# Extended-block loads issued from ScalarE's queue, the transposed inverse copied by VectorE, and new planner costs in a hybrid delta-rule encoder layer

## The chip, the cores and the metric

The kernel runs on one core of one Trainium2 chip. A core has a matrix engine (TensorE, "PE" in the profile; its weight loads are listed apart as "PEld"), three engines for elementwise work (VectorE "DVE", ScalarE "ACT", GpSimd "POOL") and SyncE ("SP"), which here does nothing but issue DMA transfers. [...] The metric is the device time of one execution in microseconds, the median of several executions. The profile is one further execution.

## What is computed

One encoder layer in fp32 on 512 tokens of width 1024: an RMS norm, one combined projection, a pooling branch, a gated delta rule run forward and backward over 8 heads, a merge by two gates, an output projection, and a feed-forward part with a width-3 convolution (inner width 2816). The change touches the delta rule. Cut to that:

```python
def gated_delta_rule(q, k, v, g, beta):      # chunks of 64 tokens, per head
    ...
    kb = k * beta[..., None]
    vb = v * beta[..., None]
    L = jnp.where(strict, jnp.einsum('bhnid,bhnjd->bhnij', kb, k) * decay, 0.0)
    rhs = jnp.concatenate([kb * jnp.exp(G)[..., None], vb], axis=-1)
    sol = lax.linalg.triangular_solve(L + eye, rhs, left_side=True, lower=True,
                                      unit_diagonal=True)
    ...
    s0 = jnp.zeros((B, H, dk, dv), jnp.float32)
    _, o = lax.scan(step, s0, xs)            # the state goes from chunk to chunk

    o_f = gated_delta_rule(qc, kc, vc, g_f, beta_f)
    flip = lambda t: jnp.flip(t, axis=1)
    o_b = flip(gated_delta_rule(flip(qc), flip(kc), flip(vc), flip(g_b), flip(beta_b)))
```

## The kernel before, in words

**Products.** Tokens lie in four tiles of 128. Every large product is fp32 split into a high and a low half: for each slab of 128 weight rows TensorE makes three products, high by high (L371), low activations by high weights (L372) and high activations by low weights (L373), each 512 columns wide. The weights come as `wr_*` blocks by DMA; ScalarE casts the high half `wh_*` (L392), GpSimd makes the low half `wl_*` (L396).

**The order.** `Planner` collects all tasks with the buffers that they read and write, a key and a cost for each engine, and simulates the engines with these costs: ring buffers come free when their last reader ends, and each engine takes the ready task with the lowest key. The simulated order becomes the program of each engine; at run time every engine goes through its own list in order and waits for semaphores. So a cost in the planner sets no duration, but it does set the order. `MM3` is the planner's cost of the three products of a slab, `FOUR` that of one group of small products in the delta rule (`pk`, `pw`, `su` and others). `L` (L273) makes a load task; all of them go to SyncE.

**The triangular solve.** The eight heads go through it in two groups of four. `inv_unit` (L863 on) inverts all 32 x 32 diagonal blocks of a group at once: the blocks are loaded as `rw`, copied as `n` (L882) and `un` (L887) by ScalarE, and thirty elimination steps run on VectorE (L897, L901), ended by a memset (L908). `back` (L912 to L914) then copies the result on ScalarE out of PSUM, `un`, into two SBUF blocks: `inv` as it stands, and `rev` with the two inner axes exchanged. Four stores (L920) put halves of them into two scratch arrays in DRAM, `u_scr` and `e_scr`. `spread_unit` (L924 on) reads them back in another layout: four loads of the extended blocks `ext` from `e_scr` and four of `nm` from `u_scr` (L941), 128 KB each. `merge_unit` (L948 on) joins the 32-wide inverses into 64-wide ones with small 32 x 32 products: `l1a` (L959) reads `nm` and `ext`, then come `l1b` (L970), `l1t` (L977) and a second level. The delta steps follow: `pw` (L1136), `su` (L1151), `o`.

Between these, the planner lets TensorE do the products of the combined projection as fillers: `ps_gd` (merge gate), `ps_k`, `ps_v`, `ps_q`, `ps_p` (pooling), `ps_gp`. Their results are convolved (`cv_*`, L747 on ScalarE, L753 on VectorE, L763 and L765 on ScalarE) or copied out (`sgd`, L1201; `pool_p`, L1290).

**The head.** `pe_warm` (L572 to L574) runs transposes of an identity that nobody reads; `spread_n1` (L563) broadcasts the norm's weights as `n1b`; `norm_transpose` (L511 on) scales (`xs`, L522) and transposes (`pt_a`, L533) a token tile.

Of the kernel before, what the change touches and what calls it, by code (L numbers as in the profile page):

```python
# [196 lines left out]
    return 0.17 + n * 0.0023  # L197


MM3, FOUR = 0.665, 0.9  # L200
TABLES = {
    "sqrt": "sqrt_and_others",
    "exp": "natural_log_exp_and_others",
# [6 lines left out]
def hybrid_block(  # L210
# [23 lines left out]
    pe, act, dve, pool, sp = nc.tensor, nc.scalar, nc.vector, nc.gpsimd, nc.sync  # L234
# [13 lines left out]
    add = plan.add  # L248
    table = {"now": "sqrt"}

    def with_table(tab, fn):
        def run():
            if table["now"] != tab:
                table["now"] = tab
                if TABLES[tab]:
                    act.preload_act_table_set(TABLES[tab])
            fn()

        return run

    def A(cost, fn, r=(), w=(), key=0.0, tab=None):
        add("act", cost, with_table(tab, fn) if tab else fn, r, w, key, tab)
# [7 lines left out]
    def M(cost, fn, r=(), w=(), key=0.0):  # L270
        add("pe", cost, fn, r, w, key)

    def L(kb, fn, r=(), w=(), key=0.0, after=(), land=Planner.LAND):  # L273
        add("sp", Planner.ISSUE, fn, r, w, key, kb=kb, after=after, land=land)

    def Z(fn, r=(), w=(), key=0.0, after=()):
        add("none", 0.0, fn, r, w, key, after=after)
# [8 lines left out]
    def bank(tag, name):  # L286
        return psum.tile([P, 512], F32, tag=tag, bufs=RINGS[tag], name=name)
# [283 lines left out]
    def pe_warm(n):  # L571
        pt = bank("ds", f"pt_warm{n}")  # L572
        for i in range(n):
            pe.transpose(pt[:, 0:P], ident, ident)  # L574
# [291 lines left out]
    def inv_unit(g):  # L866
        c = CHAIN + 1000 * g + 400
        b = {}
        fl = lambda t_: t_.rearrange("u r c -> u (r c)")
        hi_, lo_ = slice(64, 128), slice(0, 64)  # L870
        block = lambda n: ring("dp", "x4", (P, B32, B32), F32, f"{n}_{g}")

        def blocks(scr, d):
            return scr.rearrange("b h d t r c -> d (b h) t (r c)")[d]

        Z(lambda: b.update(n=block("n")), r=["pool:dp"], w=[f"x4:n{g}"], key=c)
        Z(lambda: b.update(rw=block("rw")), r=["pool:dp"], w=[f"x4:rw{g}"], key=c)
        L(256, lambda: sp.dma_start(fl(b["rw"][lo_]), blocks(b_scr[g], 0)), r=[f"bscr{g}"], w=[f"x4:rw{g}"], key=c)  # L880
        L(256, lambda: sp.dma_start(fl(b["n"][hi_]), blocks(b_scr[g], 1)), r=[f"bscr{g}"], w=[f"x4:n{g}#1"], key=c)
        A(1.1, lambda: act.copy(b["n"][lo_], b["rw"][lo_].rearrange("p r c -> p c r")),  # L882
          r=[f"x4:rw{g}"], w=[f"x4:n{g}#0"], key=c)

        def take():
            b["un"] = banks2(f"un_{g}", (P, B32, B32))
            act.copy(b["un"], b["n"])  # L887

        A(1.1, take, r=[f"x4:n{g}"], w=[f"oo:un{g}"], key=c)

        def step(k):
            un = b["un"]
            n = B32 - 1 - k
            if k == 1:
                b["tmp"] = ring("dp", "x2", (P, 256), F32, f"tmp_{g}")
            tm = b["tmp"][:, 0 : n * k].rearrange("p (r c) -> p r c", c=k)
            dve.tensor_tensor(  # L897
                out=tm, in0=b["n"][:, k + 1 :, k : k + 1].to_broadcast([P, n, k]),
                in1=un[:, k : k + 1, 0:k].to_broadcast([P, n, k]), op=ALU.mult,
            )  # L900
            dve.tensor_tensor(out=un[:, k + 1 :, 0:k], in0=un[:, k + 1 :, 0:k], in1=tm, op=ALU.add)  # L901

        for k in range(1, B32 - 1):
            V(0.44 + 2 * 0.00105 * (B32 - 1 - k) * k, lambda k=k: step(k),
              r=[f"x4:n{g}"], w=[f"oo:un{g}", f"x2:tmp{g}"], key=c)

        def end():
            dve.memset(fl(b["un"])[:, 0 : B32 * B32 : B32 + 1], 1.0)  # L908

        V(0.2, end, w=[f"oo:un{g}"], key=c)  # L910

        def back(n):  # L912
            b[n] = block(n)
            act.copy(b[n], b["un"] if n == "inv" else b["un"].rearrange("p r c -> p c r"))  # L914

        for n in ("inv", "rev"):
            A(1.1, lambda n=n: back(n), r=[f"oo:un{g}"], w=[f"x4:{n}{g}"], key=c)
        for n, rows, scr, d in (("inv", hi_, "u", 1), ("inv", lo_, "e", 0), ("rev", lo_, "u", 0), ("rev", hi_, "e", 1)):
            dst = u_scr if scr == "u" else e_scr
            L(256, lambda n=n, rows=rows, dst=dst, d=d: sp.dma_start(blocks(dst[g], d), fl(b[n][rows])),  # L920
              r=[f"x4:{n}{g}"], w=[f"{scr}scr{g}#{d}"], key=c, land=3.6)


    def spread_unit(g):  # L924
        c = CHAIN + 1000 * g + 590
        q = [slice(i * B32, (i + 1) * B32) for i in range(4)]

        def zero():
            extg[g] = ring("dp", "ext", (P, HG, 2, NT, 64), F32, f"ext_{g}")
            pool.memset(extg[g][q[0], :, 0, :, 32:64], 0.0)  # L930
            pool.memset(extg[g][q[3], :, 1, :, 0:32], 0.0)
            for h in range(g * HG, (g + 1) * HG):
                exts[h] = extg[g][:, h % HG]

        G(2.0, zero, r=["pool:dp"], w=[f"ext:{g}"], key=c)

        def load(b_, ext):
            scr = (e_scr if ext else u_scr)[g][b_].rearrange("h d t r c -> r (h d t) c")
            o = B32 * (b_ % 2)
            dst = extg[g][q[b_], :, :, :, o : o + B32] if ext else nmg[g][q[b_], :, :, :, q[b_]]  # L940
            sp.dma_start(dst.rearrange("r h d t c -> r (h d t) c"), scr)  # L941

        for b_ in range(4):
            L(128, lambda b_=b_: load(b_, True), r=[f"escr{g}", f"ext:{g}"], w=[f"exl{g}#{b_}"], key=c, land=4.0)
            L(128, lambda b_=b_: load(b_, False), r=[f"uscr{g}", f"bscr{g}", f"nm:{g}"], w=[f"nml{g}#{b_}"], key=c, land=4.0)


    def merge_unit(h):  # L948
# [445 lines left out]
        L(256, lambda: sp.dma_start(g_scr["m1"][c], b["t"]), r=[f"y:lgp{c}"], w=[f"gscrm1{c}"], key=u - 300)  # L1394


    M(4.0, lambda: pe_warm(12), w=["ds:warm0"], key=-9e6)
    A(1.3, lambda: act.preload_act_table_set("sqrt_and_others"), key=-9e6)
    for t, k in ((0, -9e6), (1, -8.9e6), (2, FEED + 240), (3, FEED + 250)):
        L(512, lambda t=t: load_x(t), w=[f"st:x{t}"], key=k)  # L1400
    L(4, load_n1, w=["st:n1"], key=-8.95e6)
    M(2.0, spread_n1, r=["st:n1"], w=["oo:n1"], key=-8.9e6)
    for t in range(NT):
        norm_transpose(
            -8e6 + t, lambda t=t: xin[t], [f"st:x{t}"], lambda: [lambda: n1["bc"][:, 0, :], lambda: n1["bc"][:, 1, :]], ["oo:n1", "oo:n1"],
            lambda: h_hi, lambda: h_lo, "h", t,
            lambda t=t: ring("st", "xs", (P, D), F32, f"xs_{t}"), f"xs:{t}", f"a{t}", None,
        )
# [8 lines left out]
    def swap_st():  # L1417
# [5 lines left out]
      after=[f"st:x{t}" for t in range(NT)] + ["st:n1", "par"] + [f"xs:{t}" for t in range(NT)])  # L1423
# [93 lines left out]
    for t in range(NT):  # L1517
        L(512, lambda t=t: sp.dma_start(x2[t], xt[t * P : (t + 1) * P, :]), r=["pool:xp"], w=[f"xr{t}#0", f"xr{t}#1"],
          key=unit["n"] * 100, after=[f"pp:do{1 + t}"])
    L(512, lambda: sp.dma_start(pools["n2b"], norm2_w[0].partition_broadcast(P)), r=["pool:xp"], w=["n2b"],  # L1520
      key=unit["n"] * 100, after=["pp:do5"])
# [48 lines left out]
    for i, (t, hf) in enumerate(order):  # L1570
        u = next_unit()
        b = {}
# [112 lines left out]
    for c in range(NF):  # L1685
        b = {}
# [275 lines left out]
```

## Time and profile before

| | us |
|---|---|
| median of three executions | 896.82 |
| lowest and highest of them | 896.58, 899.38 |
| the profiled execution | 899.88 |
| its span from first to last instruction | 898.1 |
| time outside that span | 1.78 |
| mean granted TensorE clock (1 is full) | 0.992 |

In a row of the timeline or the chain, the first number is the start in us from the start of the span and the second the duration; then come engine, line, operation, output and inputs. In brackets stands the idle time of the engine just before and what ended it. "x26" is 26 instructions of the kind in one row, and the duration then is from the first start to the last end. Matmuls overlap: the end of one is modelled and lies behind the start of the next, so TensorE's pace is read from the distance of the starts. "SPq" is SyncE's instruction queue, and the duration there is that of issuing a transfer, not that of the transfer.

### The profile page before, as it was taken

What the parts mean: (1) busy time and instruction counts of PE and PEld (TensorE: products, weight loads), DVE (VectorE), ACT (ScalarE), POOL (GpSimd) and SP (SyncE); (2) the same over time, 40 slices, a digit from 0 to 9 for tenths busy, and PEclk for the clock granted to TensorE, in tenths of its full rate; (3) what the DMA queues carried; (4) which work ended last, traced back from release to release, by engine and by line L of the source; (5) the groups of instructions that cost most, each with busy time, mean ns of one, the idle gap of its engine ahead of it and who ended that gap; (6) DMA issues with size and microseconds to landing.
All of it is one profiled execution on the core that took longest, in us unless ns stands there. A gap on an engine that the chain in (4) does not pass through costs nothing.

```text
span 898.1 us, 14074 instructions
## 1 busy us (share of the span) xinstructions
PE 880.4 (98%) x5169; PEld 739.0 (82%) x5169; DVE 551.6 (61%) x978; ACT 462.1 (51%) x791; POOL 502.7 (56%) x447
## 2 busy tenths in 40 slices
PE   8999999999999998999999999999999999999996
PEld 7888888788987886889788888888888888888885
DVE  4757596157986785555434243665655554569996
ACT  5688644345867443334864433444443333465663
POOL 3445455223665553244567905787778774567772
PEclk9999999999999998999999999999999999999998
DMA  7364446613355357112698605666666554366563
GB/s 204 96 204 128 129 119 173 132 25 105 96 141 132 115 147 126 41 48 82 203 314 283 207 26 180 210 214 208 205 226 211 199 199 124 112 199 198 168 198 117
DMA packets 176266, 140.20 MB, mean 156 GB/s; under 512 B 32111, under 2 KB 143548, under 8 KB 176197
## 3 DMA queue, kind: packets, MB, share of 16 engines
q1 hardware_dynamic: 175620, 138.25, 51.3%
q10 hardware_dynamic: 576, 1.05, 0.3%
q8 instruction: 41, 0.67, 0.3%
q14 instruction: 29, 0.23, 0.1%
HBM read 114.08 MB, written 25.20 MB: 155 GB/s over the span
## 4 chain that ended last, share of the span: by engine, by line
PE 82%; DVE 9%; DMA 3%; issue 2%; SPq 2%; ACT 1%; POOL 0%; ACTq 0%; DVEq 0%; POOLq 0%
PE ps_up L372 9%; PE ps_up L373 9%; PE ps_up L371 9%; DVE as L1630 2%; PE ps_k L371 2%; PE ps_k L372 2%; PE ps_k L373 2%; PE ps_wo L373 2%; PE pw L1136 2%; PE ps_wo L372 2%; PE ps_wo L371 2%; PE ps_z L373 2%; PE ps_do L373 2%; PE ps_do L372 2%; PE ps_z L372 2%
## 5 line engine op out<-in xcount | busy, mean ns | idle before, releaser
L396 POOL TENSOR_TENSOR wl_up<-wr_up,wh_up 128x512 fp32r<-128x512 f32 x88 | 113.4, 1310 | 51.5 <-ACT wh_up L392 51.3
L372 PE MATMUL ps_up<-h_lo,wh_up 128*128 128x512 f32 (+1 forms) x368 | 139.9, 380 | 0.3 <-DVE h_lo L541 0.3
L371 PE MATMUL ps_up<-h_hi,wh_up 128*128 128x512 f32 (+1 forms) x368 | 139.9, 380 | 0.0
L373 PE MATMUL ps_up<-h_hi,wl_up 128*128 128x512 f32 (+1 forms) x368 | 139.7, 380 | 0.0
L1676 DVE SCALAR_TENSOR_TENSOR c<-ps_up,fw,c 128x511 f32<-128x511 f32 x88 | 66.0, 750 | 100.7 <-ACT c L1670 98.8
L1661 POOL TENSOR_TENSOR tp<-tp 128x512 f32<-128x512 f32 x44 | 61.8, 1404 | 41.7 <-DMA tp<-in_ffn_down_dram 35.7
L1864 POOL TENSOR_TENSOR w_dn<-wr_dn,w_dn 128x512 fp32r<-128x512 f32 x44 | 67.5, 1550 | 26.7 <-ACT w_dn L1861 22.8
L372 PEld LDWEIGHTS ps_up<-h_lo,wh_up 128*128 128x128 f32 x368 | 69.2, 188 | 13.7 <-DVE h_lo L541 0.5
L373 PEld LDWEIGHTS ps_up<-h_hi,wl_up 128*128 128x128 f32 x368 | 69.2, 188 | 13.1
L371 PEld LDWEIGHTS ps_up<-h_hi,wh_up 128*128 128x128 f32 x368 | 69.2, 188 | 13.0
L392 ACT CAST wh_up<-wr_up 128x1024 fp32r<-128x1024 f32 x44 | 46.3, 1051 | 62.3 <-issue 22.3
L1861 ACT CAST w_dn<-wr_dn 128x512 fp32r<-128x512 f32 x69 | 42.3, 621 | 28.7 <-PE dn L373 20.2
L372 PE MATMUL dn<-w_dn,as 128*128 128x512 f32 x141 | 54.2, 385 | 0.0
L371 PE MATMUL dn<-w_dn,as 128*128 128x512 f32 x141 | 54.2, 384 | 0.0
L373 PE MATMUL dn<-w_dn,as 128*128 128x512 f32 x141 | 54.2, 384 | 0.0
L1630 DVE TENSOR_TENSOR as<-a,as 128x512 fp32r<-128x512 f32 (+1 forms) x41 | 42.3, 1057 | 0.1
L1626 ACT CAST as<-a 128x512 fp32r<-128x512 f32 (+1 forms) x41 | 21.5, 534 | 33.0 <-DVE a L1697 28.4
L396 POOL TENSOR_TENSOR wl_k<-wr_k,wh_k 128x512 fp32r<-128x512 f32 x16 | 20.1, 1282 | 29.0 <-ACT wh_k L392 25.8
L396 POOL TENSOR_TENSOR wl_gd<-wr_gd,wh_gd 128x512 fp32r<-128x512 f32 x16 | 21.5, 1368 | 25.4 <-ACT wh_gd L392 23.8
L396 POOL TENSOR_TENSOR wl_gp<-wr_gp,wh_gp 128x512 fp32r<-128x512 f32 x16 | 21.6, 1372 | 22.4 <-ACT wh_gp L392 18.0
L1670 ACT ACTIVATE c<-ps_up,fw 128x512 f32<-128x512 f32 x44 | 33.9, 770 | 0.0
L1699 ACT ACTIVATE c<-c 128x512 f32<-128x512 f32 x22 | 13.9, 633 | 35.1 <-DVE c L1676 35.1
(361 smaller groups left out, 2455.8 us busy)
## 6 DMA issues: line engine op xcount, KB each, us to landing
wr_up<-in_ffn_up_dram SPq DMA_DIRECT2D x44, 512.0 KB, 3.9
tp<-in_ffn_down_dram SPq DMA_DIRECT2D x22, 512.0 KB, 4.8
t_scr<-tp SPq DMA_DIRECT2D x44, 256.0 KB, 3.1
wr_dn<-t_scr SPq DMA_DIRECT2D x20, 512.0 KB, 3.8
wr_dn<-in_ffn_down_dram SPq DMA_DIRECT2D x15, 512.0 KB, 3.6
x<-in_x_dram SPq DMA_DIRECT2D x8, 512.0 KB, 5.3
wr_k<-in_w_in_dram SPq DMA_DIRECT2D x8, 512.0 KB, 6.0
wr_z<-in_w_in_dram SPq DMA_DIRECT2D x8, 512.0 KB, 3.8
```

What stands on the lines that cost most here:

```text
L371: pe.matmul(ps, ahi, bhi, start=first, stop=False)
L372: pe.matmul(ps, ahi, blo, start=False, stop=False)
L373: pe.matmul(ps, alo, bhi, start=False, stop=last)
L392: act.copy(b["hi"], b["raw"])
L396: pool.tensor_tensor(out=b["lo"][:, sl], in0=b["raw"][:, sl], in1=f32(b["hi"][:, sl]), op=ALU.subtract)
L1626: act.copy(sets[p][:, i : i + n, 0, :], src())
L1630: dve.tensor_tensor(out=w[:, :, 1, :], in0=src(), in1=f32(w[:, :, 0, :]), op=ALU.subtract)
L1661: G(cp(512), lambda o=o, x=x, y=y: pool.tensor_tensor(out=w(*o), in0=w(*x), in1=w(*y), op=ALU.subtract), r=[n(*x), n(*y)], w=[n(*o)], key=u)
L1670: act.activation(b[j], box["ps"], AF.Identity, scale=fw[:, 1, ci : ci + 1], bias=fw[:, 3, ci : ci + 1])
L1676: dve.scalar_tensor_tensor(out=y[:, lo:hi], in0=box["ps"][:, lo + sh : hi + sh], scalar=fw[:, k, ci : ci + 1], in1=y[:, lo:hi], op0=ALU.mu ...
L1861: act.copy(b["w"][:, 0, :], raw["t"][:, j, :])
L1864: eng.tensor_tensor(out=b["w"][:, 1, :], in0=raw["t"][:, j, :], in1=f32(b["w"][:, 0, :]), op=ALU.subtract)
```

## The change

Five edits, all in the planner's input:

- The planner's cost of the three products goes from 0.665 to 0.682 us, and `FOUR` from 0.90 to 0.88.
- `L` takes an engine and an issue cost. The four `ext` loads of each group are issued by ScalarE's queue, with a planner cost of 1.0; the four `nm` loads stay on SyncE, at 1.1 (0.45 before).
- `rev` is copied by VectorE instead of ScalarE; `inv` stays.
- `pe_warm(12)` becomes `pe_warm(13)`, with a planner cost of 2.6 instead of 4.0.
- A second `pe_warm(8)` is added, keyed between the first and the `n1b` products that it now precedes (`spread_n1` has a key of -8.9e6, but waits for the load of the weights).

```diff
-MM3, FOUR = 0.665, 0.9
+MM3, FOUR = 0.682, 0.88
...
-    def L(kb, fn, r=(), w=(), key=0.0, after=(), land=Planner.LAND):
-        add("sp", Planner.ISSUE, fn, r, w, key, kb=kb, after=after, land=land)
+    def L(kb, fn, r=(), w=(), key=0.0, after=(), land=Planner.LAND, issue=Planner.ISSUE, eng="sp"):
+        add(eng, issue, fn, r, w, key, kb=kb, after=after, land=land)
...
         def back(n):
             b[n] = block(n)
-            act.copy(b[n], b["un"] if n == "inv" else b["un"].rearrange("p r c -> p c r"))
-
-        for n in ("inv", "rev"):
-            A(1.1, lambda n=n: back(n), r=[f"oo:un{g}"], w=[f"x4:{n}{g}"], key=c)
+            if n == "inv":
+                act.copy(b[n], b["un"])
+            else:
+                dve.tensor_copy(b[n], b["un"].rearrange("p r c -> p c r"))
+
+        for n, E in (("inv", A), ("rev", V)):
+            E(1.1, lambda n=n: back(n), r=[f"oo:un{g}"], w=[f"x4:{n}{g}"], key=c)
...
-            sp.dma_start(dst.rearrange("r h d t c -> r (h d t) c"), scr)
+            (act if ext else sp).dma_start(dst.rearrange("r h d t c -> r (h d t) c"), scr)
...
-            L(128, lambda b_=b_: load(b_, True), r=[f"escr{g}", f"ext:{g}"], w=[f"exl{g}#{b_}"], key=c, land=4.0)
-            L(128, lambda b_=b_: load(b_, False), r=[f"uscr{g}", f"bscr{g}", f"nm:{g}"], w=[f"nml{g}#{b_}"], key=c, land=4.0)
+            L(128, lambda b_=b_: load(b_, True), r=[f"escr{g}", f"ext:{g}"], w=[f"exl{g}#{b_}"], key=c, land=4.0, issue=1.0, eng="act")
+            L(128, lambda b_=b_: load(b_, False), r=[f"uscr{g}", f"bscr{g}", f"nm:{g}"], w=[f"nml{g}#{b_}"], key=c, land=4.0, issue=1.1)
...
-    M(4.0, lambda: pe_warm(12), w=["ds:warm0"], key=-9e6)
+    M(2.6, lambda: pe_warm(13), w=["ds:warm0"], key=-9e6)
...
     M(2.0, spread_n1, r=["st:n1"], w=["oo:n1"], key=-8.9e6)
+    M(1.6, lambda: pe_warm(8), w=["ds:warm1"], key=-8.8e6)
```

With the new costs the planner makes a new order on every engine. The number of 512-wide products on TensorE stays the same, and ScalarE's order holds 30 loads of activation tables instead of 28. In the rows of the order below, a name's number counts up in the order in which buffers are made, `L944` in the new kernel is `L941` in the old, and `L915` is `L914`.

Where the elimination of heads 0 to 3 is prepared, ScalarE had, before the change:

```order
L763 ACTIVATE cv_v_1223<-cv_v_1223 128x512
L392 CAST wh_z_1265<-wr_z_1106 128x1024
L1189 ACTIVATE zo_1276<-ps_z_1211 128x512
L882 COPY n_376<-rw_377 64x1024
L887 COPY un_1291<-n_376 128x1024
L1077 ACTIVATE v_1296<-pt_v_1271,rki 128x128 x4
```

After it, the same engine at the same place:

```order
L392 CAST wh_q_1221<-wr_q_1075 128x1024
L747 ACTIVATE cv_v_1230<-ps_v_1164,cw 128x512
L882 COPY n_386<-rw_387 64x1024
L887 COPY un_1265<-n_386 128x1024
L392 CAST wh_z_1274<-wr_z_1147 128x1024
L1192 ACTIVATE zo_1288<-ps_z_1225 128x512
```

The two copies that VectorE's elimination needs now precede the cast of a `z` weight and the activation of its product.

Where that inverse is copied out, ScalarE had:

```order
L765 ACTIVATE qT_1574<-cv_q_1524 128x512
L914 COPY inv_1611<-un_1291 128x1024
L392 CAST wh_gd_1621<-wr_gd_1498 128x1024
L747 ACTIVATE cv_v_1634<-ps_v_1554,cw 128x512
L914 COPY rev_1640<-un_1291 128x1024
L392 CAST wh_gd_1667<-wr_gd_1547 128x1024
L1201 COPY sgd_1673<-ps_gd_1617 128x512
```

and has now:

```order
L915 COPY inv_1561<-un_1265 128x1024
L765 ACTIVATE qT_1585<-cv_q_1548 128x512
L392 CAST wh_gd_1591<-wr_gd_1466 128x1024
L1204 COPY sgd_1607<-ps_gd_1534 128x512
L944 DMA ext_391<-e_scr_101 32x32x32
L392 CAST wh_gd_1644<-wr_gd_1525 128x1024
L747 ACTIVATE cv_v_1654<-ps_v_1587,cw 128x512
L944 DMA ext_391<-e_scr_101 32x32x32 x3
L392 CAST wh_gd_1688<-wr_gd_1578 128x1024
```

`rev` has left this engine, and the four `ext` loads are issued from it, one before a weight's cast and three after the convolution behind that cast. On TensorE the first `l1a` of this group follows 498 of the 512-wide products instead of 528.

For heads 4 to 7, SyncE issued the loads before the change in this order:

```order
L387 DMA wr_gp_3459<-in_w_in_dram 128x8x128
L920 DMA e_scr_102<-rev_3443 16x4x1024
L941 DMA nm_2695<-u_scr_100 32x32x32 x3
L387 DMA wr_p_3511<-in_w_in_dram 128x8x128
L941 DMA nm_2695<-u_scr_100 32x32x32
L941 DMA ext_2118<-e_scr_102 32x32x32 x4
```

Now ScalarE has them, in these rows:

```order
L392 CAST wh_gp_3487<-wr_gp_3365 128x1024
L1293 COPY pool_p_3448<-ps_p_3436 128x512
L944 DMA ext_2056<-e_scr_102 32x32x32 x4
L392 CAST wh_p_3545<-wr_p_3417 128x1024
L1080 ACTIVATE v_3551<-pt_v_3493,rki 128x128 x4
```

The four stand between the copy of `pool_p` and the cast of the next pooling weight. The first `l1a` of this group follows 1061 wide products instead of 1067.

## What I predict

> **What bounds the kernel now.** I read the page's totals first, then the chain that ended last, then the waits of TensorE.
>
> ```profile
> span 898.1 us, 14074 instructions
> PE 880.4 (98%) x5169; PEld 739.0 (82%) x5169; DVE 551.6 (61%) x978; ACT 462.1 (51%) x791; POOL 502.7 (56%) x447
> PE 82%; DVE 9%; DMA 3%; issue 2%; SPq 2%; ACT 1%; POOL 0%; ACTq 0%; DVEq 0%; POOLq 0%
> ```
>
> TensorE is busy for 98% of the span, and the change alters neither the count nor the shape of its weight products; only small transposes at the start are added. So the time can move only where TensorE waits, where its clock is low, or where it does those transposes. The waits are few:
>
> ```profile
> PE l1a L959 <- DMA ext<-e_scr: 4.7, 4, 1.7
> ...
> PE pt_a L533 <- DVE xs L522: 0.9, 1, 0.9
> ```
>
> Of the times in each row (total, count, longest), the first is the largest: `l1a`, the first small products of the merge, waits for the extended blocks that the change loads from another queue. Around those waits the windows (length, busy time of PE, PEld, DVE, ACT, POOL, then granted clock, DMA share, GB/s) show a second loss.
>
> ```profile
> 164.00:170.00 6.00, 4.34 (x42) 3.30 (x41) 0.00 (x0) 1.80 (x3) 2.49 (x2) 0.72 1.00 243
> 344.00:355.00 11.00, 7.97 (x127) 5.44 (x126) 5.32 (x8) 2.70 (x7) 3.53 (x5) 0.69 0.77 129
> 815.00:885.00 70.00, 70.00 (x319) 58.08 (x318) 69.90 (x79) 45.48 (x85) 51.12 (x32) 1.00 0.52 167
> ```
>
> The granted clock is 0.72 and 0.69 around the two waits, and 1.00 in the down projection, where TensorE and VectorE are both full. TensorE's own rows give the size of it. Heads 0 to 3 first:
>
> ```profile
> 162.77 0.39 PE L372 MATMUL ps_gd<-h_lo,wh_gd 128*128 128x512 f32 x1
> 163.00 0.39 PE L373 MATMUL ps_gd<-h_hi,wl_gd 128*128 128x512 f32 x1
> ...
> 165.98 0.43 PE L959 MATMUL l1a<-ext,nm 32*32 32x32 f32 x26 [1.66 <-DMA ext<-e_scr]
> 166.34 0.79 PE L371 MATMUL ps_k<-h_hi,wh_k 128*128 128x512 f32 x1
> ...
> 169.07 0.63 PE L371 MATMUL ps_k<-h_hi,wh_k 128*128 128x512 f32 x1
> ...
> 169.83 0.40 PE L373 MATMUL ps_k<-h_hi,wl_k 128*128 128x512 f32 x1
> ```
>
> Starts are 0.23 us apart before the wait. The eight starts from 166.34 to 169.83 take 3.49 us where 8 x 0.23 = 1.84 would do: 1.65 us lost to the clock. Heads 4 to 7:
>
> ```profile
> 345.48 0.22 PE L959 MATMUL l1a<-ext,nm 32*32 32x32 f32 x2 [0.48 <-DMA ext<-e_scr]
> 347.20 0.32 PE L959 MATMUL l1a<-ext,nm 32*32 32x32 f32 x4 [1.50 <-DMA ext<-e_scr]
> 348.56 0.63 PE L959 MATMUL l1a<-ext,nm 32*32 32x32 f32 x26 [1.04 <-DMA ext<-e_scr]
> 349.12 0.80 PE L371 MATMUL ps_p<-h_hi,wh_p 128*128 128x512 f32 x1
> ...
> 351.98 0.49 PE L970 MATMUL l1b<-nm,x 32*32 32x32 f32 x20
> ...
> 352.88 0.80 PE L371 MATMUL ps_p<-h_hi,wh_p 128*128 128x512 f32 x1
> ...
> 354.28 0.45 PE L959 MATMUL l1a<-ext,nm 32*32 32x32 f32 x32
> ```
>
> Three waits, 0.48 + 1.50 + 1.04 = 3.02 us; then six products take 2.86 (349.12 to 351.98) instead of 1.38, and three take 1.40 instead of 0.69: 2.19 us to the clock.
>
> The Trainium skill, TensorE: Matmul & The Clock Gate, Part 1 (The HAM clock gate), speaks against the clock's share: the gate falls back only after an idle window of about 3.4 us. By that rule a pause like the first would cost its wait alone, and the sum would gain the waits without the slow stretch behind the first. The rows above disagree: after 1.66 us of waiting, eight starts take 3.49 us.
>
> **The change part by part.** *Heads 0 to 3.* Rows of ScalarE and VectorE, of the chain, and of the loads (their issue in ns, minimum, median, maximum, and the time to landing):
>
> ```profile
> 108.92 2.07 ACT L882 COPY n<-rw 64x1024 f32<-64x1024 f32 x1
> ...
> 144.42 1.01 ACT L914 COPY inv<-un 128x1024 f32<-128x1024 f32 x1 [1.50 <-DVE un L908]
> 147.11 1.05 ACT L392 CAST wh_gd<-wr_gd 128x1024 fp32r<-128x1024 f32 x1 [1.68 <-PE ps_v L372]
> 148.07 0.68 ACT L747 ACTIVATE cv_v<-ps_v,cw 128x512 f32<-128x512 f32 x1
> 148.65 1.01 ACT L914 COPY rev<-un 128x1024 f32<-128x1024 f32 x1
> 152.64 1.05 ACT L392 CAST wh_gd<-wr_gd 128x1024 fp32r<-128x1024 f32 x1 [2.99 <-PE ps_gd L372]
> ```
> ```profile
> 112.08 0.20 DVE L897 TENSOR_TENSOR tmp<-n,un 128x30 f32<-128x30 f32 x1 [6.49 <-ACT un L887]
> ...
> 144.88 1.88 DVE L1063 TENSOR_TENSOR dt<-pkq,dt 128x512 f32<-128x512 f32 x3
> ```
> ```profile
> 150.24 3.37 DMA e_scr<-rev
> ...
> 160.68 5.26 DMA ext<-e_scr
> ```
> ```profile
> L941 SPq DMA_DIRECT2D ext<-e_scr x8: 554/900/2221, 155.1 to 343.7; - x8
> ...
> DMA to landing us min/median/max: 4.2/5.1/5.5
> ```
>
> `rev` stood on ScalarE behind `inv`, a weight cast that waits for TensorE, and a convolution: it began 4.2 us after `inv`. On VectorE it follows the inverse directly. No row shows this copy there. Three 512-wide operations of VectorE take 1.88 us, so 1024 elements are 1.25 us; the bounds are ScalarE's 1.01 for the same copy and 2.07 for its transposed `n`. I take 1.25, the row of the same engine. What it delays there is VectorE's own next work, which waits on nothing that TensorE awaits at once: nothing charged.
>
> With the finish where it was, `rev` would be done at 144.4 + 1.25 = 145.7 instead of 149.7, its second store land at about 147.2 + 3.4 = 150.6, four loads at the median issue of 0.90 go until 154.2, and the last land near 159.3. But the order also puts `n` ahead of a weight's cast and its product's activation, and VectorE had waited 6.49 us for that chain before its first elimination step: I expect the inverse 2 to 6 us sooner, and the last load landed between 153 and 157. ScalarE has room to issue it: three of the four stand where `rev` was, from 148.7, before the idle 2.99 us that end at 152.64. TensorE comes to `l1a` sooner as well: 30 fewer 512-wide products stand ahead, 30 x 0.23 = 6.9 us, so it is there at 157.1 instead of 164.0. The wait is 0 at the expected finish and 2.2 with the finish where it was; I take 0, so all of it goes: **-1.66**, and with it the clock's **-1.65**. What is late next is the loads that stay on SyncE: their last was issued after the last extended one before, but four issues are gone from between them.
>
> *Heads 4 to 7.*
>
> ```profile
> 329.79 1.02 ACT L914 COPY rev<-un 128x1024 f32<-128x1024 f32 x1
> ...
> 333.85 0.58 ACT L1290 COPY pool_p<-ps_p 128x512 f32<-128x512 f32 x1
> ```
> ```profile
> 332.72 1.43 SPq L920 DMA_DIRECT2D e_scr<-rev  x1
> ...
> 339.90 4.77 SPq L941 DMA_DIRECT2D ext<-e_scr  x4
> ```
>
> Here the four extended loads were the last on SyncE, from 339.90 on. On ScalarE they stand behind the copy of `pool_p`, over at 334.4; the store of `rev` that they need, issued at 332.7 before, comes sooner with `rev`. Issued at 0.55 to 1.2 each (4.77 / 4), the last goes by 336.6 to 339.2 and lands 5.1 later, at 341.7 to 344.3. TensorE has 6 products fewer ahead, 1.4 us, so it is at `l1a` at 343.4 instead of 344.8. The wait is 0 to 0.9; I take 0: **-3.02**, and **-2.19** of clock.
>
> *The four issues on ScalarE* cost it 4 x 0.90 = 3.6 us a group. They lie beside TensorE's products as long as the casts behind them are early: the cast of 152.64 ends at 153.69, and its 24 products are the last before 164.0, so they begin near 158.5. That is 4.8 us of cover, less what GpSimd needs for the low half. I charge nothing; without that cover it would be 3.6 a group.
>
> *The head.*
>
> ```profile
> 1.63 2.82 PE L574 MATMUL pt_warm<-ident 128*128 128x128 f32 x12 [1.63 <-POOL ident masks.py:199]
> 4.38 3.78 PE L563 MATMUL n1b<-n1row,ones 1*128 1x512 f32 x4
> ...
> 9.71 1.41 DVE L522 SCALAR_TENSOR_TENSOR xs<-x,nst_a,n1b 128x512 f32<-128x512 f32 x2
> ```
>
> Twelve transposes hold TensorE from 1.63 to 4.38, 0.23 each; 21 would end 9 x 0.23 = 2.1 later, at 6.4, and the broadcast of the norm's weights starts then. If the clock is released by then, its 3.78 halves, as 3.49 against 1.84 does for products, to 1.9, and it ends at 8.3 instead of 8.2: about 0, or -0.3 where the transposes behind it gain too, for those still wait for the second tile's norm at 9.71. If not, +2.1. I take **+0.5**.
>
> *Other places.* New constants move fillers: fewer products lie between the merge of heads 0 to 3 and its delta steps, so short waits may open there. Nothing in the trace prices them; from the largest single wait left beside `l1a` (0.9 in the list above) I allow 0 to 3, three such, and take **+1.0**. The down projection has VectorE at 69.90 of 70 us and its order changes little: 0, +-1. Two more table loads stand in ScalarE's order; it is busy for 51% of the span, and they are charged at nothing.
>
> Sum: -1.66 - 1.65 - 3.02 - 2.19 + 0.5 + 1.0 = -7.0. The profiled execution took 899.88 (1.78 around the span), so 892.9 on its own basis. The median, 896.82, is 3.06 lower. If those 3.06 are part of the 1.65 + 2.19 = 3.84 of clock, which the timed runs then lost less of, they are no gain to the median, and 892.9 holds; if they lie elsewhere, the median falls by all 7.0 to 889.8. I take the middle, **891.3**.
>
> **The rivals.**
> - *The loads are still late.* The issues wait on ScalarE behind casts that themselves wait for TensorE (the 2.99 us above), and the clock falls in one group. Half of the 8.5 us of waits and clock stays, +4.3: 895.6.
> - *The transposes don't release the clock.* All nine extra are cold: +2.1 in place of +0.5, 892.9. The Trainium skill, TensorE: Matmul & The Clock Gate, Part 4 (PE-mode transpose), says that the full clock does not engage for transposes; by it this rival would hold. The trace agrees as far as twelve go (the broadcast behind them still takes 3.78 us), and shows no longer run.
> - *Slower: ScalarE becomes the bound.* If each issue holds ScalarE 2.2 us, the maximum in the row of the loads, four take 8.9, 4.1 over the cover of 4.8, in both groups +8.2; TensorE then starves for cast weights and the clock falls as before (3.84 back). From 891.3 that is 903. It decides from 1.2 us an issue (4.8 / 4) on, and breaks even with the gain near 1.9. For it: that maximum. Against it: the median of 0.90, and the idle time in front of ScalarE's casts (1.68 and 2.99 us in the rows above).
> - *The plan gives it back.* The waits go, but other waits of the new order, or VectorE's full stretch, take as much: 896.8.
>
> **How the numbers follow.** Chances: forecast 0.55, late loads 0.15, cold transposes 0.10, ScalarE as the bound 0.09, given back 0.11. A change below 0.3% (2.7 us) can't be told from none, so faster is below 894.1 and slower above 899.5. The forecast and the cold transposes give faster nearly always, the late loads a third of the time: 0.68. Given back and two thirds of the late loads give same: 0.22. Slower is 0.10. The range runs from 887.0 (896.8 less all 8.5 of waits and clock, nothing for head and fillers, 1 more from the down projection: 887.3, rounded down) to 897.0 (late loads, and given back): outside lie ScalarE's case and some small ends of the others, under 2 in 10.
>
> **What would show it.** Right: no wait of `l1a` for `ext` over 0.5 us, granted clock 1.00 around it, `rev` on VectorE near 1.3 us, issues on ScalarE near 0.9. Wrong: long ScalarE issues with casts late behind them and TensorE waiting for weights; eight starts in 3.5 us behind `l1a`; broadcast products of the head still 0.85 apart; new waits in the delta steps of heads 0 to 3. The sum fails most easily if the profiled run's 3.06 above the median is the clock that I count as gained.

## The result, and the profile after

The changed kernel takes 891.2 us in the median of six executions (889.92 to 892.58), the one before 896.7 (895.23 to 899.38): a ratio of 0.9937, 95% interval 0.9919 to 0.9955. The forecast was 891.3 in a range of 887 to 897. The profiled execution took 890.88 with a span of 889.2, so it lies 0.3 us below its median, while that of before lay 3 us above its own.

The page's totals and TensorE's waits (total, times, longest) in the changed kernel:

```profile
span 889.2 us, 14088 instructions
PE 874.7 (98%) x5178; PEld 737.1 (83%) x5178; DVE 549.0 (62%) x980; ACT 461.0 (52%) x791; POOL 497.9 (56%) x447
```
```profile
PE l1a L962 <- ACT nm L1028: 1.4, 1, 1.4
PE pt_v L778 <- ACT cv_v L763: 1.3, 1, 1.3
...
PE ps_po L371 <- DVE gpl L1395: 0.5, 1, 0.5
```

The 4.7 us for `ext` are gone from the list. Behind the 1.6 us ahead of TensorE's first instruction, which stand in both kernels, a shorter wait now leads it, for a copy of `nm` by ScalarE inside the merge of heads 4 to 7. The windows around the two places (length, busy time of five engines, granted clock, DMA share, GB/s):

```profile
157.00:164.00 7.00, 7.00 (x178) 5.11 (x175) 1.75 (x7) 4.22 (x12) 2.51 (x2) 1.00 0.50 150
...
340.00:350.00 10.00, 8.60 (x229) 6.09 (x229) 6.51 (x15) 5.53 (x15) 4.51 (x6) 1.00 0.38 105
```

The clock is 1.00 in both, where it was 0.72 and 0.69. TensorE's timeline at the first `l1a` of each group:

```profile
156.04 0.40 PE L373 MATMUL ps_gd<-h_hi,wl_gd 128*128 128x512 f32 x1
156.37 0.68 PE L962 MATMUL l1a<-ext,nm 32*32 32x32 f32 x32
156.98 0.50 PE L371 MATMUL ps_gd<-h_hi,wh_gd 128*128 128x512 f32 x1
...
339.06 0.45 PE L962 MATMUL l1a<-ext,nm 32*32 32x32 f32 x32
```

All 32 products of the first `l1a` go in one piece in both groups, with no wait. ScalarE's timeline shows the issues ("ACTq" is its queue) between its casts, and VectorE's the copy of `rev`:

```profile
145.01 0.42 ACTq L944 DMA_DIRECT2D ext<-e_scr  x1
146.32 1.05 ACT L392 CAST wh_gd<-wr_gd 128x1024 fp32r<-128x1024 f32 x1 [4.83 <-PE ps_v L372]
146.50 2.02 ACTq L944 DMA_DIRECT2D ext<-e_scr  x2
...
148.56 2.20 ACTq L944 DMA_DIRECT2D ext<-e_scr  x1
151.78 1.05 ACT L392 CAST wh_gd<-wr_gd 128x1024 fp32r<-128x1024 f32 x1 [3.83 <-PE ps_gd L372]
```
```profile
139.21 1.22 DVE L917 COPY rev<-un 128x1024 f32<-128x1024 f32 x1
```

The cast at 151.78 still waits for TensorE and not for the issues, although one of them took 2.20 us. The last `ext` is issued at 148.56, 12.1 us earlier than before (160.68).

### The profile page after: what moved, and what is told of

It reads as the page before. It is cut to its first block, busy times and chain, and to the rows that moved or that the text cites. A ratio compares the mean times of both kernels' runs of the same rounds, so it can differ in the third digit from the quotient of the medians.

```text
span 889.2 us, 14088 instructions
## 1 busy us (share of the span) xinstructions
PE 874.7 (98%) x5178; PEld 737.1 (83%) x5178; DVE 549.0 (62%) x980; ACT 461.0 (52%) x791; POOL 497.9 (56%) x447
## 4 chain that ended last, share of the span: by engine, by line
PE 92%; DVE 3%; ACT 2%; DMA 2%; issue 1%; SPq 0%; DVEq 0%; ACTq 0%
PE ps_up L372 9%; PE ps_up L371 9%; PE ps_up L373 9%; PE dn L373 3%; PE dn L371 3%; PE dn L372 3%; PE ps_k L371 2%; PE pw L1139 2%; PE o L1176 2%; PE ps_k L373 2%; PE ps_gp L371 2%; PE ps_k L372 2%; PE ps_wo L373 2%; PE ps_wo L372 2%; PE ps_wo L371 2%; PE ps_gp L372 2%
## 5 line engine op out<-in xcount | busy, mean ns | idle before, releaser
L396 POOL TENSOR_TENSOR wl_up<-wr_up,wh_up 128x512 fp32r<-128x512 f32 x88 | 115.2, 1330 | 50.1 <-ACT wh_up L392 47.9
L1665 POOL TENSOR_TENSOR tp<-tp 128x512 f32<-128x512 f32 x44 | 59.9, 1362 | 43.4 <-DMA tp<-in_ffn_down_dram 38.5
L1868 POOL TENSOR_TENSOR w_dn<-wr_dn,w_dn 128x512 fp32r<-128x512 f32 x44 | 65.6, 1504 | 29.0 <-ACT w_dn L1865 27.5
L396 POOL TENSOR_TENSOR wl_v<-wr_v,wh_v 128x512 fp32r<-128x512 f32 x16 | 20.4, 1294 | 27.5 <-ACT wh_v L392 27.5
L396 POOL TENSOR_TENSOR wl_z<-wr_z,wh_z 128x512 fp32r<-128x512 f32 x16 | 20.3, 1292 | 23.5 <-ACT wh_z L392 19.9
```

The source lines that it names most:

```text
L396: pool.tensor_tensor(out=b["lo"][:, sl], in0=b["raw"][:, sl], in1=f32(b["hi"][:, sl]), op=ALU.subtract)
L1665: G(cp(512), lambda o=o, x=x, y=y: pool.tensor_tensor(out=w(*o), in0=w(*x), in1=w(*y), op=ALU.subtract), r=[n(*x), n(*y)], w=[n(*o)], key=u)
L1868: eng.tensor_tensor(out=b["w"][:, 1, :], in0=raw["t"][:, j, :], in1=f32(b["w"][:, 0, :]), op=ALU.subtract)
```

## The experiments

Each was timed in five rounds against the kernel before on the same chip; the ratio is to that. The first four do one part of the change alone, the next three leave one part out, one keeps two parts, and three take a suspected cost away or double one. First a table of those that differ in the parts of the change alone, then each run in turn. In the table, "ScalarE" under the `ext` loads also stands for the planner's new costs of issuing these loads (1.0 and 1.1 us instead of 0.45): no run changes one without the other.

| kernel | ext loads | rev | product costs | head | ratio | 95% interval | TensorE waits for ext, us |
|---|---|---|---|---|---|---|---|
| the change | ScalarE | VectorE | new | 13+8 | 0.9937 | 0.9919 to 0.9955 | none |
| only_head | SyncE | ScalarE | old | 13+8 | 1.0003 | 0.9990 to 1.0016 | 3.9 |
| only_mm | SyncE | ScalarE | new | 12 | 1.0054 | 1.0034 to 1.0074 | 5.4 |
| only_ext | ScalarE | ScalarE | old | 12 | 0.9933 | 0.9914 to 0.9952 | none |
| only_rev | SyncE | VectorE | old | 12 | 0.9968 | 0.9956 to 0.9981 | 0.3 |
| no_ext | SyncE | VectorE | new | 13+8 | 1.0018 | 1.0006 to 1.0030 | 4.6 |
| no_mm | ScalarE | VectorE | old | 13+8 | 0.9925 | 0.9912 to 0.9937 | none |
| no_rev | ScalarE | ScalarE | new | 13+8 | 0.9936 | 0.9923 to 0.9950 | none |
| ext_rev | ScalarE | VectorE | old | 12 | 0.9927 | 0.9912 to 0.9942 | none |

Of the theories named in the expectations, Q says that the queue of the extended loads carries the gain, P that the new plan does, R that the place of `rev` does, and C that the slow stretch behind a wait is the clock's answer to the wait.

**only_head.** The kernel before, with

```diff
-    M(4.0, lambda: pe_warm(12), w=["ds:warm0"], key=-9e6)
+    M(2.6, lambda: pe_warm(13), w=["ds:warm0"], key=-9e6)
...
+    M(1.6, lambda: pe_warm(8), w=["ds:warm1"], key=-8.8e6)
```

> The kernel before with nothing but the head of the change: 13 + 8 identity transposes instead of 12; the order of every engine is otherwise that of before. Theory (the extra transposes release TensorE's clock before the broadcast of the norm's weights): the broadcast takes about 2.0 us instead of 3.8, the first token transpose starts near 8.3 instead of 9.1, and the median falls by 0.8 us, ratio 0.999. Rival (a head that ends sooner only meets a later wait): the first products start sooner, but the lead is gone by the inverse; ratio 1.000. The waits of l1a for the extended blocks stay at 4.7 us in all, give or take 1.

Measured: 896.78 us against 896.96, twelve executions against 23. TensorE's timeline of the profiled execution:

```profile
5.46 1.98 PE L563 MATMUL n1b<-n1row,ones 1*128 1x512 f32 x4
8.38 2.79 PE L533 MATMUL pt_a<-ident,xs 128*128 128x128 f32 x12 [0.93 <-DVE xs L522]
```

The mechanism is there in this execution: the broadcast takes 1.98 us and the token transposes begin at 8.38, as the theory had it. The median has none of it, as the rival had it. The rival's reason, that the lead is gone by the inverse, is not seen in this execution: TensorE reaches the first `l1a` at 163.44, 0.56 us sooner than before. The last section shows a likelier one, from other kernels with this head: not every execution gets the clock at this point. No second execution of `only_head` was traced.

**only_mm.** The kernel before, with

```diff
-MM3, FOUR = 0.665, 0.9
+MM3, FOUR = 0.682, 0.88
```

> The kernel before with nothing but the two planner costs. The new order has the inverse and its transposed copy next to each other on ScalarE, and 42 fewer wide products ahead of the first l1a, with all loads still on SyncE. Theory Q (the loads must leave SyncE's queue): SyncE issues the extended blocks about as late against l1a as before, l1a waits for them 2 us or more in all and the clock falls at least once: 894.5 to 897.5 in the median. Rival P (the plan alone makes the gain): l1a waits less than 1 us in all, clock 1.00 around it: 890.5 to 892.5.

Measured: 901.19 us, 4 to 5 us slower than before, worse than either theory had it. The waits and the windows at the two places where TensorE stood longest:

```profile
PE l1a L959 <- DMA ext<-e_scr: 5.4, 4, 2.1
PE pt_v L778 <- ACT cv_v L763: 3.6, 1, 3.6
```
```profile
268.00:280.00 12.00, 7.87 (x24) 6.21 (x25) 7.26 (x19) 8.97 (x17) 3.00 (x3) 0.72 0.47 130
...
344.00:355.00 11.00, 7.93 (x143) 5.13 (x143) 5.39 (x11) 3.35 (x8) 3.85 (x5) 0.84 0.80 146
```

The plan brings TensorE to `l1a` sooner, but SyncE's queue still issues the last extended block of heads 0 to 3 at 153.15 where the change issued it at 148.56, so the waits stay. They grow by only 0.7 us, though, and the clock around them is no lower than before. The larger new loss is the 3.6 us wait for a convolution (0.7 before), with a clock of 0.72 around it: in this order ScalarE reaches the convolution behind an activation that itself waits 3.74 us for VectorE.

**only_ext.** The kernel before, with `L`'s new arguments and

```diff
-            sp.dma_start(dst.rearrange("r h d t c -> r (h d t) c"), scr)
+            (act if ext else sp).dma_start(dst.rearrange("r h d t c -> r (h d t) c"), scr)
...
+ ... land=4.0, issue=1.0, eng="act")
+ ... land=4.0, issue=1.1)
```

> The kernel before with nothing but the extended loads on ScalarE's queue and their planner costs. inv and rev keep their places; ScalarE issues the four of heads 0 to 3 behind the activation at the old 154.1, so from 154.7 to about 158.3, landed 5.1 to 7 later at 163.4 to 165.4, and l1a is reached 3 products later than before, at 164.7. Theory Q: at most 0.7 us of wait is left in heads 0 to 3 and at most 2 in heads 4 to 7 (three of four are issued behind the cast at the old 338.7, landed near 347 against TensorE at about 347): 891 to 894. Rival P: most waits stay, 895 to 897.

Measured: 890.36 us, the whole gain of the change by this part alone. No wait for `ext` is left in TensorE's list, ScalarE issues the last blocks of heads 0 to 3 sooner than SyncE did (160.68), and the clock is 1.00 at both places:

```profile
155.19 2.98 ACTq L941 DMA_DIRECT2D ext<-e_scr  x2
```
```profile
164.00:170.00 6.00, 6.00 (x130) 4.07 (x129) 0.87 (x3) 2.73 (x7) 2.52 (x2) 1.00 0.91 213
341.00:352.00 11.00, 11.00 (x166) 8.27 (x164) 4.24 (x11) 4.50 (x9) 7.33 (x8) 1.00 0.81 126
```

Here `rev` is still on ScalarE and its place is the old one: it did not have to move. P falls with this run and the one before it.

This part is itself two: the queue, and the planner's higher costs for the issues, which change the order. Ahead of the first `l1a`, the order of `only_ext` has 3 more wide products than before in heads 0 to 3 and 15 more in heads 4 to 7. At 0.23 us each that is 0.7 us against a wait of 1.66, and 3.5 us against waits of 3.02. So in heads 0 to 3 the later `l1a` covers less than half of the wait, and the sooner issue the rest; in heads 4 to 7 the later `l1a` could cover all of it with the loads where they were. The loads on SyncE under the higher costs were not run, and what the queue is worth by itself stays open.

**only_rev.** The kernel before, with `rev` copied by `dve.tensor_copy` and planned on VectorE.

> The kernel before with nothing but the transposed copy on VectorE. rev is done near 145.6 instead of 149.7, all loads stay on SyncE, and l1a comes 12 wide products (2.7 us) sooner. Theory Q: rev was not what the loads waited for last; of the 4 us the loads gain at most 3 and l1a's lead takes 2.7 of it, so the waits of heads 0 to 3 stay within 1 us of before: 894.5 to 897.5. Rival R (the place of rev is the cause): the waits are gone, 890 to 893.

Measured: 894.0 us, between the ranges of Q and R; both miss. TensorE's list has

```profile
PE pt_v L778 <- ACT cv_v L763: 1.3, 1, 1.3
PE ps_do L371 <- ACT wh_do L392: 1.1, 1, 1.1
PE l1a L962 <- ACT nm L1028: 1.0, 1, 1.0
...
PE ps_do L373 <- POOL wl_do L396: 0.6, 1, 0.6
...
PE l1a L962 <- DMA ext<-e_scr: 0.3, 1, 0.3
```

Q had the waits of `l1a` stay, and they went, from 4.7 to 0.3 us: in this plan `rev` came early enough for the loads on SyncE too. R had all of the gain follow, and only half of it did. The waits for `cv_v` and for `nm` stand in the change's list as well; those for weights of the delta rule's output projection (`ps_do`, 1.7 us in all) don't, and are a part of the 3 us or so that are missing. Where the rest went is open. So the two moves are two ways of removing the same wait, and each is enough for that under the old costs of the products.

**no_ext.** The changed kernel with the extended loads on SyncE.

```diff
-            (act if ext else sp).dma_start(dst.rearrange("r h d t c -> r (h d t) c"), scr)
+            sp.dma_start(dst.rearrange("r h d t c -> r (h d t) c"), scr)
```

> The changed kernel with the extended loads back on SyncE, the other parts of the change kept. Theory Q (the queue of these loads is what counts; it alone gave 890.4): l1a waits 2 us or more for the blocks in all, the clock falls behind at least one of the waits, as with the two planner costs alone (5.4 us of waits, 901.2): 896 to 902. Rival P2 (the new plan with rev on VectorE makes up for the queue, since rev alone gave 894.0): waits below 1 us, 890 to 893.5.

Measured: 899.48 us, as Q had it: the whole gain is lost, and a little more. Waits, and the window of heads 4 to 7:

```profile
PE l1a L962 <- DMA ext<-e_scr: 4.6, 3, 2.8
PE pt_v L778 <- ACT cv_v L763: 3.6, 1, 3.6
```
```profile
342.00:352.00 10.00, 6.48 (x125) 4.42 (x124) 4.64 (x9) 3.01 (x8) 3.98 (x5) 0.83 0.79 137
```

Under the new costs of the products `rev` on VectorE no longer makes up for the rest. In heads 0 to 3 TensorE is at `l1a` 6.6 us earlier than in `only_rev` (154.66 against 161.28), and the last block is issued only 5.5 us earlier. In heads 4 to 7, where 3.5 of the 4.6 us are waited, the last block is issued 5.2 us later than there and TensorE comes 2.3 us later. Not all of the loss is at `l1a`: the 3.6 us wait for the convolution is back, 2.3 us longer than in the change. As in `only_ext`, the queue and the costs of the issues change together: the order of `no_ext` has 9 and 21 fewer wide products ahead of the two `l1a` than that of the change, 2.1 and 4.8 us of work.

**no_mm.** The changed kernel with `MM3, FOUR = 0.665, 0.9`.

> The changed kernel with the planner's costs of products as before (0.665 and 0.90), the other parts kept. Theory Q: no wait of l1a for the blocks over 0.5 us, 889.5 to 891.5, no slower than the change, since the costs bring nothing of the gain. Rival (the costs are needed to place the loads on ScalarE and to bring the inverse forward): waits of 1 us or more at l1a, above 893.

Measured: 890.95 us, ratio 0.9925, level with the change, as Q had it. The costs bring none of the gain.

**no_rev.** The changed kernel with `rev` on ScalarE, which this plan puts right behind `inv`:

```profile
137.76 1.03 ACT L914 COPY rev<-un 128x1024 f32<-128x1024 f32 x1
```

> The changed kernel with rev back on ScalarE, where this plan puts it right behind inv; the other parts kept. Theory Q: rev ends at most 1.5 us later than in the change in heads 0 to 3 and sooner or level in heads 4 to 7, the loads on ScalarE are still in time: 890.3 to 892.2, within 0.2% of the change. Rival R (rev's engine carries part of the gain also here): above 893.

Measured: 892.1 us, ratio 0.9936 against the change's 0.9937, as Q had it. ScalarE even has `rev` done by 138.8, before VectorE starts it in the change (139.21).

**fill_wait.** The kernel before, with work for TensorE put into the wait:

```diff
             a, z = slice(0, 32), slice(32, 64)
+            for i in range({0: 20, HG: 32}.get(h, 0)):
+                pe.transpose(b["p1"].rearrange("p t c -> p (t c)"), ident, ident)
             for t in range(NT):
```

> The kernel before with 20 and 32 identity transposes put ahead of the first l1a of heads 0 to 3 and 4 to 7, into the bank that l1a then overwrites; everything else and every order is as before. TensorE is so kept at work for about 2.2 and 3.5 us while the blocks are on their way. Theory C (the slow stretch behind l1a is the clock's answer to the wait): the granted clock stays at 1.00 around both places, eight products behind the first l1a take 1.8 to 2.0 us instead of 3.5, and the profiled run ends 2.5 to 4 us sooner than the 899.88 of before, while the median falls by 0.5 to 2, since most timed runs lose less clock than that profiled one. Rival (the slow stretch comes with the small products or the transfers, whatever TensorE does meanwhile): the clock falls as before, and the time is the same or up to 1 us longer.

Measured: 895.56 us against 898.14, ratio 0.9973 (0.9962 to 0.9983); seven executions between 895.05 and 895.71, where 17 of before on that chip spread from 894.35 to 899.49. TensorE's timeline at heads 0 to 3:

```profile
164.28 2.35 PE L958 MATMUL l1a<-ident 128*128 128x128 f32 x20
166.56 0.45 PE L961 MATMUL l1a<-ext,nm 32*32 32x32 f32 x32
166.94 0.50 PE L371 MATMUL ps_k<-h_hi,wh_k 128*128 128x512 f32 x1
...
168.90 0.39 PE L373 MATMUL ps_k<-h_hi,wl_k 128*128 128x512 f32 x1
```

The blocks are no sooner there than before, but eight starts (166.94 to 168.90) take 1.96 us instead of 3.49. The windows 164 to 170 and 344 to 355 show a clock of 1.00. So the slow stretch is the clock's answer to TensorE standing still, and C holds; the rival, that it comes with the small products or the transfers, falls. The clock's part of the median is about 2.4 us (0.27%), somewhat more than expected.

**ext_rev.** The kernel before with only the loads and `rev` moved.

> The kernel before with the extended loads on ScalarE's queue and rev on VectorE; head and planner costs of products as before. Theory Q: like the run without the planner costs, whose head alone differs (ratio 0.9925): ratio 0.991 to 0.994, no wait of l1a for the blocks over 0.5 us. Rival (the second set of transposes in the head is worth 0.8 us after all): 0.1% above that run, which the interval can't settle, but its first gate product would start at or after 12.6 in the profile in most executions.

Measured: 889.92 us, ratio 0.9927. Its head is the slow one of the expectation's rival (first gate product at 12.65), and still it is not behind `no_mm`.

**hold_head.** As `ext_rev`, with

```diff
-    M(4.0, lambda: pe_warm(12), w=["ds:warm0"], key=-9e6)
+    M(2.6, lambda: pe_warm(13), w=["ds:warm0"], key=-9e6)
...
+    M(1.6, lambda: pe_warm(14), r=["oo:n1"], w=["ds:warm1"], key=-8.8e6)
```

> As ext_rev, but with 13 identity transposes ahead of the broadcast and 14 behind it, which read its result's place only as an order. Theory C (a pause of TensorE lets the clock fall, and work holds it): the pause of 0.9 us between the broadcast and the first token transpose is filled, the 16 token transposes start 0.11 us apart instead of 0.21, and the first gate product starts 0.3 to 1.2 us sooner than in ext_rev; the median is up to 1 us lower, ratio 0.990 to 0.993. Rival (token transposes are slow for another reason): still 0.21 apart, and the time level with ext_rev.

Measured: 891.32 us, ratio 0.9941 (0.9925 to 0.9958); no better, and the expectation misses:

```profile
1.63 3.04 PE L574 MATMUL pt_warm<-ident 128*128 128x128 f32 x13 [1.63 <-POOL ident masks.py:199]
4.59 3.78 PE L563 MATMUL n1b<-n1row,ones 1*128 1x512 f32 x4
8.30 3.25 PE L574 MATMUL pt_warm<-ident 128*128 128x128 f32 x14
11.35 1.91 PE L533 MATMUL pt_a<-ident,xs 128*128 128x128 f32 x8
```

In this execution TensorE works from 1.63 on without a pause and is still at the slow pace at 11.35 (14 transposes in 3.05 us, 0.22 each); the pause was not what kept it there.

**all8_act.** The changed kernel with the `nm` loads on ScalarE's queue as well.

```diff
-            (act if ext else sp).dma_start(dst.rearrange("r h d t c -> r (h d t) c"), scr)
+            act.dma_start(dst.rearrange("r h d t c -> r (h d t) c"), scr)
...
+ ... w=[f"nml{g}#{b_}"], key=c, land=4.0, issue=1.0, eng="act")
```

> The changed kernel with the four nm loads of each group on ScalarE's queue too, so eight issues a group there instead of four. Theory Q with the cover of the prediction (some 4 us of ScalarE's idle time in front of the next casts): eight issues of 0.9 to 1.1 us take 7 to 9 us a group, so 0 to 4 us a group beyond the cover; the casts are late and TensorE waits for weights for 0 to 4 us in all: 891 to 897. Rival R3 (an issue on ScalarE holds it at the maximum of 2.2 us, and each late cast also costs clock): 898 or more. If the issues cost nothing at all there, 891, level with the change.

Measured: 894.86 us, ratio 0.9978 (0.9967 to 0.9989), some 3.7 us slower than the change and inside the first range. ScalarE's timeline of heads 4 to 7:

```profile
336.95 0.31 ACTq L944 DMA_DIRECT2D ext<-e_scr  x1
337.30 0.58 ACTq L944 DMA_DIRECT2D nm<-u_scr  x1
341.62 0.31 ACTq L944 DMA_DIRECT2D ext<-e_scr  x1
...
342.65 0.63 ACT L763 ACTIVATE cv_v<-cv_v 128x512 f32<-128x512 f32 x1 [4.66 <-DMA nm<-u_scr]
```

Most single issues are short (medians of 0.31 and 0.58 us). But with eight of them the engine stands for 4.66 us until the last pair is out, and the convolution and the cast behind it come later; TensorE's longest wait is then 1.8 us for the copy of `nm` by ScalarE. That is the slower rival's mechanism, begun but not at its price: no weight is waited for. Nor is all of the time shown to come from it. Of the 4.6 us between the two profiled executions, 2.7 are there at the first gate product (14.57 against 11.89), before any of these loads, since this execution's head was slow (last section).

## Why the prediction was right, by its steps

**The waits for the extended blocks (-1.66 and -3.02).** Right in size and place: both are gone. The steps there were rougher. The inverse came 8.4 us sooner (`inv` at 136.06 instead of 144.42) where 2 to 6 were expected, and the blocks took 7.1 us to land instead of 5.1; the two errors offset each other. The last block of heads 0 to 3 landed near 155.7 (148.56 + 7.1), within the forecast 153 to 157 and 0.7 us ahead of `l1a`. `only_ext` and `no_ext` show that this part of the change carries the gain under either set of product costs. They don't show how much of it is the queue and how much the order that the higher issue costs make; the prediction gave the planner's issue costs no term.

**The clock behind them (-1.65 and -2.19).** Right in the profiled execution, where both windows now read 1.00, and shown to be the clock by `fill_wait`. The doubt about the median was right too: the profiled execution of before lost 3.84 us to it, the median 2.4. That accounts for nearly half of the 5.6 us by which the median fell (0.63% of 896.7). With the 4.7 us of waits, and 1.3 us of waits that opened elsewhere (below), the sum is 5.8 us; this takes the waits of the profiled executions for those of the median.

**`rev` on VectorE.** The 1.25 us were right (1.22 measured). Its weight in the argument was not: the prediction put part of the gain down to `rev` and to the earlier inverse. `no_rev` shows that under the new costs it may stay on ScalarE, and `only_ext` that the old place is early enough for loads on ScalarE.

**The four issues on ScalarE.** "I charge nothing" held, though single issues took up to 2.20 us: the casts behind them still waited for TensorE (3.83 us at 151.78). With twice as many (`all8_act`) ScalarE does stand behind its issues, and the kernel is slower; how much of that the issues cost isn't parted from the head.

**The head (+0.5).** The term failed in sign in the profile: token transposes begin at 8.33 instead of 9.09, so -0.76. The step behind it assumed that all 21 transposes run at 0.23 us; they took 3.79 us (1.63 to 5.42), as the last eight ran at about half of that. In the median it is 0 (`only_head`, 1.0003).

**Other places (+1.0).** Mis-sized by little in sum. Besides the head and `ext`, TensorE's list of before had

```profile
PE ps_po L371 <- DVE gpl L1392: 0.7, 1, 0.7
PE pt_v L778 <- ACT cv_v L763: 0.7, 1, 0.7
PE pms L1248 <- DVE nm L847: 0.5, 1, 0.5
```

as its largest waits, 1.9 in all; now the three largest are 1.4, 1.3 and 0.5, so 1.3 more. ScalarE's timeline ahead of the 1.3 us wait, and at the same place before the change:

```profile
263.35 1.28 ACT L763 ACT_TABLE_LOAD   x1
264.64 0.63 ACT L763 ACTIVATE cv_v<-cv_v 128x512 f32<-128x512 f32 x1
```
```profile
270.02 1.28 ACT L763 ACT_TABLE_LOAD   x1
```

A table load of 1.28 us stands between TensorE and the convolution that it waits for, but in both kernels, so it isn't one of the two that were added. Those are among the four loads from 226.01 to 243.16, where the kernel before has two (231.57 and 241.38). TensorE doesn't stand still in that stretch and its clock is 1.00: "charged at nothing" held.

**The median.** The forecast took the middle between 892.9 and 889.8; 891.2 came out. The agreement to 0.1 us is luck: the head was off by 0.5 to 1.3 us, the clock's share of the median was a guess halfway, and the interval of the ratio is 3 us wide. Between the profiled executions, where no such guess is needed, the sum of 7.0 us was 2.0 too small (899.88 to 890.88). The head gave 1.3 us more than forecast and the other places took 0.3 more, so 1.0 us is not assigned.

**The costs of the products.** The prediction gave them only the +1.0. `only_mm` shows what was not foreseen: alone they make the kernel 4 to 5 us slower. The waits for `ext` have only a small part in it (5.4 us instead of 4.7); most is the 3.6 us wait for a convolution and the slow clock behind it. In the change that wait is 1.3 us; which part of the change shortens it was not shown beyond `no_ext`, where it is 3.6 again. `no_mm` and `ext_rev` (0.9925 and 0.9927) do without them and are no slower than the change; their advantage of 0.1% is inside the intervals.

## What to carry to other kernels

Where an engine that is busy for 98% waits a little for a load, count what the wait costs behind it as well: here 4.7 us of waiting drew up to 3.8 us of slow clock after it, and the second part can be had by itself with filler work. When several edits aim at one wait, do each alone: one of four carried the gain, one was a second way to half of it, one was nothing, and one was a loss that didn't show beside the first. Where one edit changes both where a task runs and what the planner believes that it costs, do these apart as well, since the cost alone moves other work.

## What was not expected of the hardware

**The clock at the start comes at no fixed time.** With 21 transposes, TensorE's pace doubled during them in five profiled executions (the change, `only_head`, `no_ext`, `no_mm` and `no_rev`), but not in that of `all8_act`. With twelve it stayed slow in five, and doubled in that of `only_ext`, whose broadcast took 2.29 us instead of 3.78. The granted clock doesn't tell these apart: it reads 1.00 at the start of all of them, though the same transposes go 0.23 us apart there and 0.11 apart in `fill_wait`. The timeline of `all8_act`, behind that of the change:

```profile
1.63 3.86 PE L574 MATMUL pt_warm<-ident 128*128 128x128 f32 x21 [1.63 <-POOL ident masks.py:199]
5.42 1.98 PE L563 MATMUL n1b<-n1row,ones 1*128 1x512 f32 x4
8.33 2.79 PE L533 MATMUL pt_a<-ident,xs 128*128 128x128 f32 x12 [0.93 <-DVE xs L522]
```
```profile
1.63 4.74 PE L574 MATMUL pt_warm<-ident 128*128 128x128 f32 x21 [1.63 <-POOL ident masks.py:199]
6.30 3.78 PE L563 MATMUL n1b<-n1row,ones 1*128 1x512 f32 x4
11.01 3.50 PE L533 MATMUL pt_a<-ident,xs 128*128 128x128 f32 x16 [0.93 <-DVE xs L522]
```

The same instructions end 2.7 us later there. Nine more transposes so gain 0.8 us against the old head or lose 1.9 (11.01 against 9.09), and the median shows neither. Over the profiled executions the first gate product starts at 12.54 us in the mean of the six with 21 transposes (11.89 to 14.57), and at 12.61 in the mean of the six with twelve: the two heads are level. What decides between the two was not found. The Trainium skill, TensorE: Matmul & The Clock Gate, Part 4 (PE-mode transpose), says that transposes don't bring the full clock; the change's row speaks against it as a rule, since the pace doubled while nothing but transposes ran, while the rows of `hold_head` and `all8_act` agree with it.

**How long a pause the clock bears.** It fell behind waits of 1.66 us before and, in `no_ext`, 2.8 us, and not behind 1.26 and 1.41 us in the change. Length alone doesn't decide: in the change's head the granted clock reads 0.50 from 8.4 to 11.0 us, after a pause of 0.93 us that follows the broadcast, and the token transposes there are slow again (twelve in 2.79 us). The other five executions with a fast broadcast show the same. Whether the pause or the broadcast's four products, with one row of input each, brought it was not tried. The Trainium skill, on the same page, Part 1 (The HAM clock gate), names an idle window of about 3.4 us; here a pause of half that was enough, in some executions and not in others: the executions of before lie between 894.35 and 899.86 us, and those with work in the pause within 0.66 us of one another. The clock that is listed with each execution bears this out: of 57 executions of before, the twelve with a mean granted clock of 0.998 or more took 894.35 to 896.39 us, and the sixteen with 0.992 or less 897.54 to 899.86.
